# Seven products of combined halves in the output projection, with the combinations formed during the second half of the prompt, and a later place for DeltaNet's doubling

## The chip, the cores and the metric

The kernel runs on one core of one Trainium2 chip. TensorE (PE) multiplies and has its own weight loads (PEld); VectorE (DVE), ScalarE (ACT) and GpSimd (POOL) do the rest; transfers are issued from two queues, SyncE's (SP) and ACT's. The metric is the time of one execution in microseconds (us). Three runs of the kernel before took 2514.7, 2506.16 and 2504.16 us, median 2506.16; the profiled execution took 2504.23 us, with a span of 2502.5 us.

## What is computed

One decoder layer on a prompt of 1024 tokens (with 16 meta tokens in front) and on 64 sample tokens (8 sequences of 8), width 2048, in float32:

```python
h = _rmsnorm(x, norm_w)
proj = jnp.einsum('bld,de->ble', h, w_in)          # 2048 x 8984: all q, k, v, gates, z
# 16 heads of 128: 6 mLSTM (A), 6 gated DeltaNet (B), 4 HGRN2 (C); each a scan over chunks with a state
hcat = jnp.concatenate([ha, hb, hc], axis=2)
hcat = hcat * lax.rsqrt(jnp.mean(hcat * hcat, axis=-1, keepdims=True) + EPS)     # per head
y = hcat.reshape(bsz, L, MIX) * out_norm_w * jax.nn.silu(z)
out = jnp.einsum('ble,ed->bld', y, w_out)          # 2048 x 2048
return x + out, (states ...)                        # then a last _rmsnorm with final_norm_w
```

DeltaNet needs a triangular solve of 64x64 in each chunk: `lax.linalg.triangular_solve(M, rhs, left_side=True, lower=True)`.

## The kernel before

**Products in float32.** Every factor is split in two parts, hi (cast to fp32r) and lo (the rest), and a product is three matmuls: hi x hi, lo x hi, hi x lo. A weight is loaded in pieces of 128x512 (256 KB) on ACT's DMA queue into `wraw` (5 buffers); ACT casts `whi`, DVE subtracts `wlo`. `next_piece` hands out a piece, `feed_ahead` splits three pieces ahead and loads seven ahead. A piece serves 12 matmuls of 512 columns in the second half.

**Stages.** The prompt is done in two halves of 512 tokens. Half 0 holds also the 64 samples and the meta tokens. For each half the input projection runs through all heads in the order of `ORDER` (tiles `acc`, from `hA` or `hB`); as the tiles of a head are done, `done_tile` starts the head's scan. Scan matmuls go on PE between the projection's. At a head's end `finish` takes the head norm (`hr`, with a power on POOL), multiplies with `silu(z)` (`zs`), splits `y` into hi and lo and stores both in DRAM (`y_dram`). The output projection stands behind the second half's input projection: for half 0 four groups of 512 columns, 16 heads each, four token tiles and the samples; then half 1 the same. Its accumulators are `oacc`. `load_y` reads `y` back; the residual `x` is added from tiles `res`, squares are summed on ACT, POOL multiplies with `fnw` (the final norm's weights), and `final_norm` scales and stores the rows, among the following group's matmuls.

**What sets the order.** The order of the program is written by a planner of the kernel's own. A `Clock` holds an estimated time for each engine; `Weave` holds queues of generators, `scan`, `fin` (finishes), `post` and `bg`. Between two matmuls of a projection `pump` lets the heads of the queues go on whose due time has come by PE's clock T. `drain` moves T forward until some streams are done. `start_head` keeps at most two heads open: for the next it drains the oldest one's scan and all finishes in the queue. A scheduler then lays the instructions out engine by engine; each engine works in that order and waits for semaphores. All engine operations are recorded in one helper, L137, so they are told apart by tiles.

**DeltaNet.** `gdn_scan` builds `Ball` (decay times k k), writes its diagonal blocks to DRAM (`db`, eight transfers on SP, L1209) and reads them back spread over the partitions (`Bb`, three transfers, L1215). On DVE the substitution works on the 16x16 blocks: 15 pairs `Yt<-Yc,Bb` and `Yc<-Yc,Yt`, then `Y`, transposed to `X`. The doubling follows, from 16 to 32 to 64 and beyond: `pz<-X,Ball` on PE, an evacuation to `s`, `pyy<-Y,s` on PE, a subtraction, the next stage. The planner puts the substitution at `ready` = T + 7 us or later and the doubling 8 us behind the substitution's end.

## Time and profile before

| | |
|---|---|
| runs | 2514.7, 2506.16, 2504.16 us |
| profiled execution | 2504.23 us, span 2502.5 us |
| PE busy | 2439.2 us (97%) |
| DVE, ACT, POOL busy | 58%, 40%, 22% |
| moved | 350.81 MB, mean 140 GB/s |
| output projection | from about 2100 us to the end, 1664 matmuls |

The page names engines, tiles and, behind "<-", what ended an idle time. PE's share of 97% means that PE's order and its waits set the time; other engines count where PE waits for them.

### The profile page before, as it was taken

What the parts mean: (1) busy time and instruction counts of PE and PEld (TensorE: products, weight loads), DVE (VectorE), ACT (ScalarE), POOL (GpSimd) and SP (SyncE); (2) the same over time, 40 slices, a digit from 0 to 9 for tenths busy, and PEclk for the clock granted to TensorE, in tenths of its full rate; (3) what the DMA queues carried; (4) which work ended last, traced back from release to release, by engine and by line L of the source; (5) the groups of instructions that cost most, each with busy time, mean ns of one, the idle gap of its engine ahead of it and who ended that gap; (6) DMA issues with size and microseconds to landing.
All of it is one profiled execution on the core that took longest, in us unless ns stands there. A gap on an engine that the chain in (4) does not pass through costs nothing.

```text
span 2502.5 us, 43732 instructions
## 1 busy us (share of the span) xinstructions
PE 2439.2 (97%) x16032; PEld 2182.3 (87%) x16032; DVE 1439.8 (58%) x3080; ACT 992.7 (40%) x2428; POOL 553.6 (22%) x743
## 2 busy tenths in 40 slices
PE   6989999999999999999999999999999999999998
PEld 5988999999999999998787888888888888888886
DVE  7775665764647656555854556554654546333435
ACT  5733434443434334343642334333533334222324
POOL 5331212421204312123320114110320102111201
PEclk9999999999999999999999999999999999999999
DMA  6656666655545445448445455454544559536735
GB/s 149 159 128 154 159 151 150 161 121 124 129 104 140 99 124 138 105 111 227 121 122 119 117 124 131 120 133 101 142 119 112 132 124 308 135 82 203 248 101 181
DMA packets 681043, 350.81 MB, mean 140 GB/s; under 512 B 260004, under 2 KB 622076, under 8 KB 680828
## 3 DMA queue, kind: packets, MB, share of 16 engines
q10 hardware_dynamic: 318528, 185.64, 29.4%
q1 hardware_dynamic: 362300, 162.37, 25.1%
q8 instruction: 126, 2.06, 0.3%
q14 instruction: 89, 0.73, 0.1%
HBM read 285.71 MB, written 62.19 MB: 139 GB/s over the span
## 4 chain that ended last, share of the span: by engine, by line
PE 78%; DVE 7%; DMA 6%; issue 3%; ACT 2%; POOL 2%; SPq 2%; ACTq 0%; DVEq 0%; POOLq 0%
PE acc L137 54%; PE oacc L137 13%; DVE wlo L137 2%; PE pa L137 1%; SPq L1209 1%; DMA wraw<-in_w_in_dram 1%; DMA Bb<-db 1%; PE po L137 1%; PE pyy L137 1%; PE nd L137 1%; PE pu L137 1%; PE pz L137 1%; DVE Yt L137 1%; PE poh L137 1%; DVE Yc L137 1%
## 5 line engine op out<-in xcount | busy, mean ns | idle before, releaser
L137 DVE TENSOR_TENSOR wlo<-wraw,whi 128x512 fp32r<-128x512 f32 x720 | 536.8, 747 | 559.4 <-ACT whi L137 527.0
L137 PE MATMUL acc<-hA,whi 128*128 128x288 f32 (+1 forms) x4544 | 821.0, 303 | 5.3 <-DVE whi L137 5.1
L137 ACT CAST whi<-wraw 128x512 fp32r<-128x512 f32 x720 | 443.6, 618 | 945.4 <-PE acc L137 463.3
L137 PE MATMUL acc<-hB,whi 128*128 128x512 f32 x2272 | 724.8, 401 | 3.8 <-DMA hB<-hblo 3.3
L137 PEld LDWEIGHTS acc<-hA,whi 128*128 128x128 f32 x4544 | 676.1, 190 | 10.4 <-issue 6.9
L137 PEld LDWEIGHTS acc<-hB,whi 128*128 128x128 f32 x2272 | 414.9, 190 | 86.4 <-DMA hB<-hblo 4.0
L137 PE MATMUL acc<-hA,wlo 128*128 128x288 f32 x2240 | 487.9, 298 | 2.0 <-DVE wlo L137 1.8
L137 PE MATMUL acc<-hB,wlo 128*128 128x512 f32 x1120 | 441.0, 394 | 1.3 <-DVE wlo L137 1.3
L137 PEld LDWEIGHTS acc<-hA,wlo 128*128 128x128 f32 x2240 | 365.7, 189 | 3.3 <-DVE wlo L137 3.3
L137 PE MATMUL oacc<-whi,y 128*128 128x512 f32 x1088 | 343.0, 390 | 1.0 <-ACT whi L137 1.0
L137 PEld LDWEIGHTS acc<-hB,wlo 128*128 128x128 f32 x1120 | 211.5, 189 | 49.1 <-DVE wlo L137 3.6
L137 PEld LDWEIGHTS oacc<-whi,y 128*128 128x128 f32 x1088 | 204.3, 188 | 43.7 <-ACT whi L137 1.7
L137 PE MATMUL oacc<-wlo,y 128*128 128x512 f32 x576 | 224.7, 390 | 2.0 <-DVE wlo L137 2.0
L137 PEld LDWEIGHTS oacc<-wlo,y 128*128 128x128 f32 x576 | 108.2, 188 | 25.6 <-DVE wlo L137 3.6
L137 POOL TENSOR_TENSOR res<-res,fnw 128x512 f32<-128x512 f32 (+1 forms) x34 | 48.6, 1457 | 258.1 <-ACT oscr L137 258.1
L137 POOL TENSOR_TENSOR y<-y,zs 128x592 fp32r<-128x592 f32 (+1 forms) x32 | 45.9, 1435 | 155.5 <-ACT zs L137 152.6
L137 POOL TENSOR_TENSOR qd<-qT,emb 128x512 f32<-128x512 f32 x12 | 17.8, 1480 | 232.3 <-PE po L137 232.3
L137 DVE TENSOR_TENSOR Yt<-Yc,Bb 128x60 f32<-128x60 f32 (+8 forms) x180 | 36.9, 205 | 46.2 <-DMA Bb<-db 40.9
L137 POOL TENSOR_TENSOR hr<-hr,halfneg 128x4 f32<-128x4 f32 (+1 forms) x48 | 46.5, 969 | 67.4 <-DVE hr L137 66.1
L137 POOL TENSOR_TENSOR nrm<-nrm,halfneg 128x10 f32<-128x10 f32 x12 | 23.4, 1954 | 143.4 <-DVE nrm L137 126.8
L137 POOL TENSOR_TENSOR X<-Ex,hk 128x256 f32<-128x256 f32 (+1 forms) x40 | 41.4, 1035 | 56.6 <-PE pa L137 48.2
L137 DVE TENSOR_TENSOR Sx<-Sx,lf 128x256 f32<-128x256 f32 (+2 forms) x60 | 36.3, 609 | 23.1 <-ACT Ex L137 21.2
(416 smaller groups left out, 2755.5 us busy)
## 6 DMA issues: line engine op xcount, KB each, us to landing
wraw<-in_w_in_dram ACTq DMA_DIRECT2D x564, 256.0 KB
wraw<-in_w_out_dram ACTq DMA_DIRECT2D x144, 256.0 KB
y<-y SPq DMA_DIRECT2D x16, 576.0 KB
px<-in_x_prompt_dram SPq DMA_DIRECT2D x32, 256.0 KB
yd<-y SPq DMA_DIRECT2D x128, 64.0 KB
out_dram<-sst SPq DMA_DIRECT2D x16, 512.0 KB
s<-yd SPq DMA_DIRECT2D x32, 256.0 KB
y<-zs SPq DMA_DIRECT2D x32, 256.0 KB
```

The costliest lines, as they stand in the source:

```text
L137: return f(out, *a, **k)
L1209: DMA(db[j], Ball[SUB * j:SUB * (j + 1), 0:C, SUB * j:SUB * (j + 1)])
```

## The change

The output projection is done as one product of 2x2 blocks in the form of Strassen and Winograd. The rows' blocks are the two halves of the prompt, the columns' blocks column groups 0, 1 and 2, 3, and the inner blocks two sets of eight heads: K1, the first eight in the order of the input projection, and K2. There are seven products, numbered 1 to 7 here: A11·B11, A12·B21, S2·T2, S1·T1, S4·B22, S3·T3, A22·T4. Each has two column groups, eight pieces and four tiles; the samples, which are computed plainly, go along in the first three. Partial sums are held in tiles `t1` and `q`, copied and added by ACT, DVE and POOL, and the residuals are added on POOL in `x_added`.

The S are sums and differences of `y` of both halves. `finish` of half 0 also stores `y` whole; `finish` of half 1 loads this, forms the combinations on POOL, splits each on ACT and DVE, and stores them: three stores for a head of K1 (and one load), eight for a head of K2 (and three loads). The T are combinations of blocks of `w_out`. A background stream in half 1, `combine_weights`, forms them in 16 rounds: four loads of 256 KB on SP, which are kept behind all that precedes them in the source, four subtractions on POOL, four stores to DRAM on SP. `gdn_scan`'s two numbers rise from 7 to 10 and from 8 to 11.

Counted over the program, PE has 10809 rows (before 10951), POOL 795 (692), SP 850 (593), DVE 2728 (2643).

```diff
-OUT_UNITS = ([(cg, range(5)) for cg in range(4)], [(cg, range(4)) for cg in range(3)] + [(3, range(2)), (3, range(2, 4))])
+HEADS = [{"A": 0, "B": HA, "C": HA + HB}[name[0]] + int(name[1]) for name in ORDER[1:]]
+K1, K2 = HEADS[:NH // 2], HEADS[NH // 2:]
+LAST_UNITS = [(0, range(4)), (1, range(2)), (1, range(2, 4))]
...
+        if not half.first:
+            DMA(ya, y_whole[0][K1[kk]])
+            if not upper:
+                DMA(yb, y_whole[1][kk])
+                DMA(yc, y_whole[0][head])
...
+        if half.first:
+            S.copy(yhi[:, 0:W], y[:, 0:W])
+            ck.last += 1.0
+            yield
+            DMA(y_whole[0][head], y[:, 0:HALF])
+            ck.last = ck.t["T"] + 2.0
+            yield
+            G.tensor_tensor(ylo[:, 0:W], y[:, 0:W], yhi[:, 0:W], op=ALU.subtract)
...
+        def parts(src, hi, name):
+
+            S.copy(hi, src)
+            ck.sync()
+            V.tensor_tensor(src.bitcast(F32R), src, hi, op=ALU.subtract)
+            d = y_comb[name][kk].bitcast(F32)
+            ck.last = max(ck.last, ck.t["T"]) + 3.0
+            yield
+            DMA(d[:, 0:HALF], hi.bitcast(F32))
+            DMA(d[:, HALF:], src)
+
+        if upper:
+            G.tensor_tensor(ya, ya, y, op=ALU.subtract)
+            ck.last += 1.0
+            yield
+            DMA(y_whole[1][kk], y)
+            yield from parts(ya, yhi, "S3")
+            return
+        G.tensor_tensor(yb, yb, y, op=ALU.add)
+        yield
+        yield from parts(y, yhi, "A22")
+        G.tensor_tensor(ya, yb, ya, op=ALU.subtract)
+        yield
+        yield from parts(yb, spare, "S1")
...
-        ready = ck.t["T"] + 7.0
+        ready = ck.t["T"] + 10.0
...
-        ck.last += 8.0
+        ck.last += 11.0
...
+    def combine_weights():
+        for j in range(2):
+            for kk in range(NK // 2):
+                b11, b12, b21 = (sp.tile([P, 512], F32, tag="px", name="px", bufs=3) for _ in range(3))
+                b22 = sp.tile([P, 512], F32, tag="pxs", name="pxs", bufs=1)
+                for t, heads, cg in ((b11, K1, j), (b12, K1, j + 2), (b22, K2, j + 2), (b21, K2, j)):
+                    tc.keep_in_program_order(DMA(t, i["w_out"][0, P * heads[kk]:P * (heads[kk] + 1), 512 * cg:512 * (cg + 1)]))
+                for dst, a, b in ((b11, b12, b11), (b12, b22, b12), (b22, b22, b11), (b21, b21, b22)):
+                    ck.last = ck.t["T"] + 7.0
+                    yield
+                    G.tensor_tensor(dst, a, b, op=ALU.subtract)
+                ck.last = ck.t["T"] + 4.0
+                yield
+                for n, t in (("T1", b11), ("T3", b12), ("T2", b22), ("T4", b21)):
+                    DMA(w_comb[n][NK // 2 * j + kk], t)
+                ck.last = ck.t["T"] + 10.0
+                yield
...
+    each = every(0, "S4")
+    for j in range(2):
+        accs = banks()
+        phase(1, j, accs, halfn, each=each)
+        for n in halfn:
+            q[j, n] = free.pop(0)
+            ck.begin()
+            V.tensor_tensor(q[j, n], t1[j, n], accs[n], op=ALU.add)
+    weave.drain_queue("post")
+
+    each = every(1, "S3", [x_rows((4, 12), 1, 2), x_added(t1, 5, 0)])
+    for j in range(2):
+        accs = banks()
+        phase(0, j, accs, halfn, each=each)
+        for n in halfn:
+            t = res[n + 1, j + 2]
+            ck.begin()
+            V.tensor_tensor(t, t, accs[n], op=ALU.add)
+            G.tensor_tensor(t, t, q[j, n], op=ALU.add)
+            squared(n + 1, j + 2)
+    weave.add("post", final_norm(range(1, 5), range(4)))
...
```

The last two pieces are products 5 (S4) and 6 (S3).

How the instructions move shows at three places. The first is the doubling of DeltaNet's fifth head (B4) in half 1. On PE, before and then with the change (a name's number is its buffer; `acc` rows are the input projection of the heads behind):

```order
L137 MATMUL acc<-hB_14959,wlo 128x512
L137 MATMUL pz<-X_21883,Ball 32x32 x16
L137 MATMUL acc<-hB_14959,whi 128x512
L137 MATMUL acc<-hB_14960,whi 128x512
L137 MATMUL acc<-hB_14959,wlo 128x512
L137 MATMUL pyy<-Y_21882,s_22081 32x32 x16
L137 MATMUL acc<-hB_14743,whi 128x512
L137 MATMUL acc<-hB_14744,whi 128x512
L137 MATMUL acc<-hB_14743,wlo 128x512
L137 MATMUL acc<-hB_14743,whi 128x512
L137 MATMUL acc<-hB_14744,whi 128x512
L137 MATMUL acc<-hB_14743,wlo 128x512
```

```order
L137 MATMUL acc<-hB_14984,wlo 128x512
L137 MATMUL pz<-X_22222,Ball 32x32 x16
L137 MATMUL pyy<-Y_22221,s_22332 32x32 x16
L137 MATMUL pz<-X_22222,Ball 32x32 x8
L137 MATMUL pyy<-Y_22221,s_22378 32x32
L137 MATMUL pyy<-s_22378,Y_22221 32x32
...
L137 MATMUL pyy<-Y_22221,s_22378 32x32 x4
L137 MATMUL pz<-s_22358,Ball 64x64 x4
L137 MATMUL pyy<-s_22356,s_22427 64x64 x4
L137 MATMUL acc<-hB_14772,whi 128x512
L137 MATMUL acc<-hB_14773,whi 128x512
L137 MATMUL acc<-hB_14772,wlo 128x512
```

Before, three to eighteen `acc` matmuls stand between two stages; now the stages follow each other directly, up to the last `pyy`. On DVE at the same place, from the substitution's end, before and then with the change:

```order
L137 TENSOR_TENSOR Y_21882<-Yc,evenodd 128x128
L137 STREAM_TRANSPOSE X_21883<-Y_21882 128x128
L137 COPY Yc<-subid 128x64
L137 TENSOR_TENSOR wlo<-wraw,whi 128x512 x2
L137 TENSOR_TENSOR s_22081<-pz,lowleft 128x4x32
L137 STREAM_TRANSPOSE vT<-acc 128x512
L137 TENSOR_TENSOR Y_21882<-Y_21882,pyy 128x128
L137 TENSOR_TENSOR wlo<-wraw,whi 128x512
L137 STREAM_TRANSPOSE X_21883<-Y_21882 128x128
L137 TENSOR_TENSOR s_22105<-Y_21882,submask 128x512
L137 TENSOR_TENSOR wlo<-wraw,whi 128x512
L137 TENSOR_SCALAR s_22105<-pyy 32x4x32
```

```order
L137 TENSOR_TENSOR Y_22221<-Yc,evenodd 128x128
L137 STREAM_TRANSPOSE X_22222<-Y_22221 128x128
L137 COPY Yc<-subid 128x64
L137 TENSOR_TENSOR s_22332<-pz,lowleft 128x4x32
L137 TENSOR_TENSOR Y_22221<-Y_22221,pyy 128x128
L137 STREAM_TRANSPOSE X_22222<-Y_22221 128x128
L137 TENSOR_TENSOR s_22356<-Y_22221,submask 128x512
L137 TENSOR_SCALAR s_22356<-pyy 32x4x32
L137 TENSOR_SCALAR s_22358<-pyy 32x4x32
L137 TENSOR_SCALAR s_22356<-pyy 32x4x32
L137 TENSOR_SCALAR s_22356<-pyy 64x4x64
L137 SCALAR_TENSOR_TENSOR s_22240<-pr,cols,s_22240 128x128
```

The splits `wlo` of the projection's pieces, which stood between the stages, are ahead of them or behind them now. The second place is SP ahead of DeltaNet's first head (B0) in half 1, before and then with the change (`yd`, `y`, `yw`, `S` and `ya` belong to the finish of the head before, `T` are the stores of a round of combinations):

```order
L812 DMA yd_16185<-y 32x16x32 x4
L816 DMA s_16181<-yd_16185 128x4x128
L879 DMA y_767<-zs 128x512
L879 DMA y_767<-y 128x512
L1209 DMA db_16351<-Ball 64x1x16 x8
L785 DMA nm<-rows_765 128x512
L1215 DMA Bb<-db_16351 128x1x384 x2
L1215 DMA Bb<-db_16351 128x1x192
L785 DMA bb<-rows_765 128x512
```

```order
L844 DMA s_19076<-yd_19080 128x4x128
L1775 DMA T_82<-px 128x512
L1775 DMA T_84<-px 128x512
L1775 DMA T_83<-pxs 128x512
L1775 DMA T_85<-px 128x512
L948 DMA yw_92<-y 128x512
L941 DMA S_88<-zs 128x512
L942 DMA S_88<-ya 128x512
L899 DMA ya<-yw_91 128x512
L1289 DMA db_19301<-Ball 64x1x16 x8
L813 DMA nm<-rows_776 128x512
L1295 DMA Bb<-db_19301 128x1x384 x2
```

Four stores of combinations, which wait for POOL, and four transfers of the longer finish now stand ahead of `db`, where two stores stood. The third place is PE at an mLSTM head of half 0, before and then with the change:

```order
L137 MATMUL acc<-hA_88,wlo 128x288
L137 MATMUL acc<-hA_88,wlo 128x304
L137 MATMUL pot<-ident,tho 80x128
L137 MATMUL pum<-meta_731,kwall 128x137
L137 MATMUL pum<-s_5268,kwall 128x129 x4
L137 MATMUL acc<-hA_88,whi 128x288
L137 MATMUL acc<-hA_88,whi 128x304
L137 MATMUL acc<-hA_89,whi 128x288
L137 MATMUL acc<-hA_89,whi 128x304
L137 MATMUL acc<-hA_88,wlo 128x288
L137 MATMUL acc<-hA_88,wlo 128x304
```

```order
L137 MATMUL acc<-hA_99,wlo 128x304
L137 MATMUL pot<-ident,tho 80x128
L137 MATMUL pum<-meta_742,kwall 128x137
L137 MATMUL pum<-s_5305,kwall 128x129 x4
L137 MATMUL py<-ident,t_5210 128x80
L137 MATMUL nd<-sst,spread_740 32x129 x8
L137 MATMUL nd<-t_5294,t_5252 32x129 x2
L137 MATMUL nd<-t_5294,t_5252 16x129
L137 MATMUL nd<-state_A_758,qd 128x129
L137 MATMUL nd<-s_5305,s_5260 128x129
```

Where `pum` and `nd` had `acc` matmuls between them, they now follow each other; six heads of half 0 have this with the change, two had before.

338 lines of the change are left out of this document (243 added, 95 removed).

## The prediction

> **What bounds the kernel now.** I read the page first: the busy shares, the slices, and the shares of the chain of waits.
>
> ```profile
> PE 2439.2 (97%) x16032; PEld 2182.3 (87%) x16032; DVE 1439.8 (58%) x3080; ACT 992.7 (40%) x2428; POOL 553.6 (22%) x743
> ...
> PE   6989999999999999999999999999999999999998
> ...
> DMA  6656666655545445448445455454544559536735
> GB/s 149 159 128 154 159 151 150 161 121 124 129 104 140 99 124 138 105 111 227 121 122 119 117 124 131 120 133 101 142 119 112 132 124 308 135 82 203 248 101 181
> ...
> PE 78%; DVE 7%; DMA 6%; issue 3%; ACT 2%; POOL 2%; SPq 2%; ACTq 0%; DVEq 0%; POOLq 0%
> PE acc L137 54%; PE oacc L137 13%; DVE wlo L137 2%; PE pa L137 1%; SPq L1209 1%; DMA wraw<-in_w_in_dram 1%; DMA Bb<-db 1%; PE po L137 1%; PE pyy L137 1%; PE nd L137 1%; PE pu L137 1%; PE pz L137 1%; DVE Yt L137 1%; PE poh L137 1%; DVE Yc L137 1%
> ```
>
> TensorE (PE) is busy for 2439.2 of 2502.5 us, no slice after the second falls below 9 tenths, and the chain runs through PE for 78%. So a matmul taken away is worth its time, and anything new costs only if PE waits for it. In the output projection the groups of instructions and the windows say what one matmul is worth:
>
> ```profile
> L137 PE MATMUL oacc<-whi,y 128*128 128x512 f32 x1088 | 343.0, 390 | 1.0 <-ACT whi L137 1.0
> ...
> L137 PE MATMUL oacc<-wlo,y 128*128 128x512 f32 x576 | 224.7, 390 | 2.0 <-DVE wlo L137 2.0
> ```
>
> ```profile
> core 0: us, PE busy (x) PEld busy (x) DVE busy (x) ACT busy (x) POOL busy (x), PEclk, DMA share, GB/s
> 2000.00:2100.00 100.00, 100.00 (x583) 82.59 (x582) 48.16 (x113) 35.28 (x76) 9.16 (x13) 1.00 0.67 190
> 2100.00:2200.00 100.00, 100.00 (x503) 83.80 (x502) 45.55 (x70) 34.08 (x72) 25.02 (x23) 1.00 0.61 176
> 2200.00:2300.00 100.00, 100.00 (x443) 82.84 (x442) 32.79 (x44) 26.68 (x53) 14.54 (x10) 1.00 0.44 134
> 2300.00:2400.00 100.00, 98.73 (x435) 81.08 (x434) 40.39 (x70) 31.33 (x60) 16.92 (x14) 1.00 0.67 214
> ```
>
> The columns are the stretch, its length, busy time (and instructions) of PE, weight load, DVE, ACT and POOL, then the clock, the DMA share and GB/s. Between 2200 and 2300 us there is nothing but the output projection: 443 matmuls in 100 us, 0.2257 us each (the 390 ns of the groups overlap). It waits for almost nothing (1.0 and 2.0 us in the two groups). The waits of PE that the change touches:
>
> ```profile
> PE pz L137 <- DVE Yc L137: 4.0, 1, 4.0
> ...
> PE pz L137 <- DVE X L137: 2.7, 1, 2.7
> ...
> PE oacc L137 <- DVE wlo L137: 2.0, 3, 1.5
> ...
> PE nd L137 <- DVE nsT L137: 0.5, 1, 0.5
> ```
>
> **Part 1: fewer matmuls.** Before, the projection has 1088 + 576 = 1664. The seven products have 7 x 2 x 8 pieces x 4 tiles x 3 = 1344, the samples 128: 1472. 192 x 0.2257 = **-43.3 us**. All else on PE keeps its count.
>
> **Part 2: the doubling is placed later.** The two waits of `pz` (3.98 and 2.70 us, the first DeltaNet head of each half) are longer than they look, for the clock falls behind them:
>
> ```profile
> 225.00:230.00 5.00, 3.25 (x40) 3.05 (x40) 4.78 (x16) 1.14 (x2) 0.00 (x0) 0.64 0.44 108
> 230.00:235.00 5.00, 4.87 (x47) 4.53 (x46) 3.20 (x10) 2.01 (x7) 1.71 (x3) 0.50 0.80 136
> 235.00:240.00 5.00, 5.00 (x65) 4.51 (x64) 2.68 (x7) 1.78 (x7) 1.09 (x4) 0.83 0.22 56
> ...
> 1330.00:1335.00 5.00, 5.00 (x42) 4.01 (x41) 1.86 (x4) 0.28 (x1) 0.87 (x2) 0.50 0.38 96
> 1335.00:1340.00 5.00, 5.00 (x58) 3.44 (x57) 2.07 (x5) 1.14 (x3) 0.00 (x0) 0.92 0.19 22
> ```
>
> At clocks 0.50 and 0.83 the windows from 230 to 240 us lose 5 x 0.50 + 5 x 0.17 = 3.35 us; those from 1330 to 1340 lose 2.9. The planner now places the doubling 3 us later (+8 to +11). For head B0 of half 0 that takes 3.0 of 3.98 us and, with a wait near 1 us left, the clock's loss: 3.0 + 3.4 = **-6.4 us** (bounds 0 and -7.4). For head B0 of half 1 it would take 2.7 + 2.9 = 5.6 us, but the order shows a round of the weights' combinations ahead of its `db` rows on SP. Before, POOL and SP stood there so:
>
> ```profile
> 1298.35 1.96 POOL L137 TENSOR_TENSOR nrm<-nrm,halfneg 128x10 f32<-128x10 f32 x1 [11.00 <-DVE nrm L137]
> ```
>
> ```profile
> 1306.74 5.07 SPq L1209 DMA_DIRECT2D db<-Ball  x8
> ...
> 1314.07 1.90 SPq L1215 DMA_DIRECT2D Bb<-db  x3
> ```
>
> The four subtractions stand behind that `nrm` operation, which ends at 1300.3. Each costs what the nearest POOL row of 128x512 costs (the first row here):
>
> ```profile
> L137 POOL TENSOR_TENSOR res<-res,fnw 128x512 f32<-128x512 f32 (+1 forms) x34 | 48.6, 1457 | 258.1 <-ACT oscr L137 258.1
> ...
> L137 DVE TENSOR_TENSOR Yt<-Yc,Bb 128x60 f32<-128x60 f32 (+8 forms) x180 | 36.9, 205 | 46.2 <-DMA Bb<-db 40.9
> ```
>
> 1300.3 + 4 x 1.46 = 1306.1 us, when T4's store is released. Behind it on SP stand three stores of the head before and one load; the stores wait for one more POOL subtraction (1.5), a cast and a DVE subtraction (some 1.4). So `db` starts near 1310.5 instead of 1306.74, and `Bb` 3.8 us later. That eats the 3.4 us that `pz` moved back: **0** (bounds -5.6, if SP gets through, and +4, if a load lands late).
>
> **Part 3: head B4 of half 1.** The finishes of half 1 have become longer, and the planner's clock, which is made to wait for the oldest head, jumps just when this head's substitution runs. The order shows the result: `pz` and `pyy` stand in one block with no `acc` matmul between them, and the two rows of `wlo` that stood between the substitution's end and `s<-pz` before are gone, as are all up to the end of the doubling. Counted in the program from the first `Yt`, 56 matmuls (12.7 us) stood ahead of `pz` before and 11 (2.5 us) do now. Before, the trace has there:
>
> ```profile
> 2010.40 0.22 DVE L137 TENSOR_TENSOR Yt<-Yc,Bb 128x60 f32<-128x60 f32 x1 [4.20 <-DMA Bb<-db]
> ...
> 2018.99 0.31 DVE L137 STREAM_TRANSPOSE X<-Y 128x128 f32<-128x128 f32 x1
> ...
> 2021.64 0.28 DVE L137 TENSOR_TENSOR s<-pz,lowleft 128x128 f32<-128x128 f32 x1
> ```
>
> ```profile
> 2020.61 0.90 PE L137 MATMUL pz<-X,Ball 32*32 32x32 f32 x32
> ...
> 2022.32 0.89 PE L137 MATMUL pyy<-Y,s 32*32 32x32 f32 x32
> ...
> 2025.42 0.59 PE L137 MATMUL pz<-X,Ball 32*32 32x32 f32 x16
> ...
> 2031.83 0.68 PE L137 MATMUL pyy<-s,s 64*64 64x64 f32 x8
> ```
>
> X was ready at 2018.99 + 0.31 = 2019.30 and `pz` began at 2020.61, 1.3 us of slack. With 10.2 us less ahead of it PE waits 10.2 - 1.3 = 8.9 us. Then come five hand-offs without cover. From `pz` at 2020.61 the evacuation began 1.03 us later, took 0.28, and `pyy` followed 0.4 us behind it: some 1.7 us for a pair in which PE works 0.9. With ACT's and POOL's copies in the later ones I take 0.9 us of idle PE each, 4.7 in all. An idle of 9 us also costs clock: by the two instances above, 3.4 us. Sum **+17.0 us**. Bounds: 8 (Bb there at once, no loss of clock) and 25 (1.5 us a hand-off, DVE's splits between, 5 us of clock).
>
> The Trainium skill (TensorE: Matmul & The Clock Gate, Why this matters for your kernels) says to keep gaps of PE under about 3 us, or the clock drops to half. The trace agrees and is harsher: the 2.70 us wait already brought 0.50. By the rule only B4's first wait costs clock, which is what I took; without the rule the sum would be 3.4 us lower.
>
> **Part 4: half 0.** Finishes yield twice more and write `y_whole`. On PE six of the mLSTM heads now have `pot`, `pum`, `nd`, `pu` with no `acc` between, two before. The rows of such a wait are 0.5 us (`nd <- nsT`): 4 to 5 more of them, **+2.5 us** (0 to 5). The 16 more stores lie on SP, and nothing waits for them before half 1.
>
> **Part 5: weights' combinations.** 64 loads, 64 stores and 64 subtractions in half 1: 33.5 MB in some 1000 us, 34 GB/s beside the 101 to 142 of those slices: hidden. 64 x 1.46 = 93 us on POOL, busy 22%. What costs is order: each round holds POOL for the loads plus 5.8 us, and SP until then. Of the other `db` rows none has a round within 8 us ahead. DVE waits for POOL's powers in `finish`, but these are off PE's path until the planner drains. **+2 us** (0 to 10).
>
> POOL's work also slows DVE's split:
>
> ```profile
> 2084.96 0.69 DVE L137 TENSOR_TENSOR wlo<-wraw,whi 128x512 fp32r<-128x512 f32 x1 [2.03 <-ACT whi L137]
> ...
> 2089.34 1.37 DVE L137 TENSOR_TENSOR wlo<-wraw,whi 128x512 fp32r<-128x512 f32 x1 [1.21 <-DMA wraw<-in_w_out_dram]
> ```
>
> ```profile
> 2088.87 1.30 POOL L137 TENSOR_TENSOR y<-y,zs 128x512 fp32r<-128x512 f32 x1 [16.62 <-ACT zs L137]
> ```
>
> The split takes 0.69 us alone and 1.37 under a POOL operation. With 103 more POOL rows that is at most 70 us of DVE, busy 58%, and splits are made three pieces (8.1 us) ahead: nothing on the path. The Trainium skill (GPSIMD Engine Reference, 8. Key points) names the cause, SBUF interfaces shared with VectorE. Taken as a price on the path, 64 x 0.68 = 44 us, it would eat the whole saving; I don't, because `oacc` waited 2.0 us for `wlo` in all while POOL was busy 25 us in 100.
>
> **Part 6: the output stage's epilogue.** Behind products 5 and 6 POOL has 12 operations for a column pair, 17.5 us against 192 / 2 x 0.2257 = 21.7 us. DVE's scaling of the rows of tiles 1 to 4 waits for POOL's power, and the split of a later piece stands behind it; the cover is 8.1 us. I take **+4 us** (0 to 12) for this, the six banks of a column pair of product 2, and the end.
>
> **Part 7: transfers.** Products 1 to 3 (704 matmuls, 158.9 us) read 80 pieces (21.0 MB), S2 and S1 (8.4), x (2.1), and the last heads' finishes move some 8.6: 40.1 MB, 252 GB/s. The windows show 214 GB/s at a share of 0.67 and 176 at 0.61, so 290 to 320 at 1.0, and one slice had 308 while PE didn't wait. It fits, with little room: **+2 us** (0 to 20).
>
> Sum: -43.3 - 6.4 + 0 + 17.0 + 2.5 + 2 + 4 + 2 = -22.2. The profiled execution took 2504.2 us, 1.9 below the median: 2482.0 there, **2484 us** as a median.
>
> **Rivals.** *No jam at B4*: the runtime order absorbs it (Bb earlier, DVE free of splits). For: DVE has no splits to do there. Against: PE's order is fixed. Without the 17.0: 2467 us. *The output stage runs at the speed of DMA*: at 240 GB/s the 40.1 MB take 167 us, at 220 182: 8 to 23 us, less the 2 counted: about 2498. For: before, this stage never had more than 214 over 100 us. Against: the 308 slice. *The epilogue binds*: POOL's column pairs leave 4 us; if splits wait at each of three, 12 us instead of 4: 2492. *The combinations hold SP and POOL ahead of DeltaNet*: one mechanism at each `Bb` of half 1. If loads land 8 us late, the store rows hold SP as at B0, and all six heads stall 3 us more and lose 3 us of clock: 2484 + 38 = 2522. It decides from the point where a round ends later than its `db`'s place; the rows give the other five 8 us or more. *The change doesn't do what it says*: the order has the 192 matmuls less, so this has no weight.
>
> **How the numbers follow.** Forecast 0.45, no jam 0.20, DMA 0.13, epilogue 0.12, SP and POOL 0.10. About 0.5% (12.5 us) is what a measurement here can tell from no change, so faster means below 2493.6. The forecast's own range is 2472 to 2496; nearly all of it, the no-jam case and half of the epilogue's are faster: 0.70. DMA, the rest of the epilogue's and of the forecast's are within: 0.21. Slower: 0.09. The range for 8 in 10 reaches from the no-jam case (2467, with epilogue and transfers free 2461) into the DMA case's upper end: 2461 to 2507.
>
> **What would show it.** Right: 0.226 us per matmul in the products; a wait of `pz` for DVE of 7 to 11 us in half 1's fifth DeltaNet head, with the clock at 0.5 behind it; no such wait in the first head of half 0; one of 2 to 4 us still in the first head of half 1; `Bb` issued some 4 us later there. Wrong: `oacc` waiting for DMA or `wlo` by more than 10 us in products 1 to 3; POOL's subtractions ahead of a DeltaNet wait elsewhere; `pz` at B4 without a wait.

## The result: slower by 2.4%

The changed kernel takes 2566.48 us (median of 2563.59, 2563.84, 2569.11 and 2571.99), the kernel before, beside it, 2509.39 us: a ratio of 1.0239 (95% interval 1.0220 to 1.0258), 57 us slower. The forecast was 2484, its range 2461 to 2507. Both miss, and on the other side.

The profiled execution of the changed kernel took 2571.99 us, the longest of the four. Its page, in the parts that answer those shown of before:

```profile
PE 2435.8 (95%) x15840; PEld 2164.0 (84%) x15840; DVE 1525.0 (59%) x3160; ACT 1022.8 (40%) x2476; POOL 711.6 (28%) x855
...
PE   6989999999999999998999999999987999899988
...
PE 22%; DMA 5%; DVE 3%; issue 3%; POOL 3%; ACT 1%; SPq 1%; ACTq 0%; POOLq 0%; DVEq 0%
```

PE has fewer instructions (15840 for 16032) but is busy as long as before (2435.8 and 2439.2 us): what is left runs at a lower clock. There are slices of 8 tenths in the second half. The chain of waits can't be compared: followed back from the end it breaks off at 1558 us, so its shares add up to 38% of the span, and PE's 22% is not to be held against the 78% of before. PE's four largest groups of waits (behind each the total, the count and the longest; before, `oacc` waited 2.0 us for `wlo`):

```profile
PE acc L137 <- DVE wlo L137: 16.3, 15, 2.4
PE pz L137 <- DVE X L137: 14.7, 3, 11.9
PE pyy L137 <- DVE s L137: 11.5, 8, 2.6
PE oacc L137 <- DVE wlo L137: 11.2, 6, 5.6
```

Two kinds stand out: DVE's splits `wlo`, in the input projection and in the output projection (27.5 us), and DeltaNet's `pz` and `pyy` (26.2 us), with the longest single wait. To see where the time went I cut the span at the first `acc` matmul of half 1 behind half 0's last scan matmuls (80 of half 1's 3392 have run by then), at the last `acc`, and at the last `oacc`. "Waits" is PE's idle time in the stage.

| us | half 0 | half 1 | output stage | waits in each |
|---|---|---|---|---|
| before | 1202.0 | 898.4 | 391.2 | 44.8, 5.0, 3.0 |
| after | 1208.1 | 970.0 | 380.9 | 53.4, 46.5, 23.6 |

Half 1 lost 71.6 us. The output stage won 10.3 where 43.3 were due. A stage of a single execution is good to some 6 us: the changed kernel and ten of the kernels below have the same order on PE up to half 1's first `acc` matmul, and their half 0 took from 1203.2 to 1215.2 us. The windows that hold half 1 and most of the output stage, and two short ones that are used further down, of after and then of before (columns as in the prediction):

```profile
1208.10:2178.10 970.00, 923.54 (x4986) 749.85 (x4985) 549.04 (x1091) 364.43 (x840) 262.69 (x253) 0.96 0.62 170
2178.10:2490.00 311.90, 290.48 (x1291) 237.00 (x1290) 161.89 (x237) 112.76 (x219) 100.17 (x80) 0.97 0.77 249
2140.00:2200.00 60.00, 60.00 (x284) 50.44 (x283) 34.97 (x60) 26.56 (x52) 18.32 (x18) 1.00 0.91 309
2380.00:2440.00 60.00, 60.00 (x267) 49.67 (x266) 25.02 (x35) 14.32 (x24) 14.96 (x11) 1.00 0.72 232
```

```profile
1202.00:2100.40 898.40, 893.35 (x4985) 738.44 (x4984) 505.52 (x1064) 351.96 (x818) 161.07 (x183) 0.99 0.52 131
2100.40:2490.00 389.60, 386.59 (x1760) 319.50 (x1759) 164.61 (x248) 127.23 (x251) 72.21 (x59) 1.00 0.55 168
```

Half 1 has 46.5 - 5.0 = 41.5 us more of waits, and the same matmuls kept PE busy for 923.54 us instead of 893.35, 30.2 longer: that is the whole loss. The longer busy time goes with the clock, whose mean fell from 0.99 to 0.96: 0.04 x 970.0 - 0.01 x 898.4 = 30 us (good to some 5 us, since the clock is printed to two digits and some of the low clock falls into the waits themselves). The output stage likewise: 391.2 - 43.3 = 347.9, plus 20.6 of waits, plus some 11 of clock (0.97 for 1.00), makes 380; 380.9 were measured. So there is one question: what are the waits? In half 1 each costs about 1.7 times its length.

### The profile page after: what moved, and what is told of

It reads as the page before. It is cut to its first block, busy times and chain, and to the rows that moved or that the text cites. A ratio compares the mean times of both kernels' runs of the same rounds, so it can differ in the third digit from the quotient of the medians.

```text
span 2570.1 us, 44178 instructions
## 1 busy us (share of the span) xinstructions
PE 2435.8 (95%) x15840; PEld 2164.0 (84%) x15840; DVE 1525.0 (59%) x3160; ACT 1022.8 (40%) x2476; POOL 711.6 (28%) x855
## 5 line engine op out<-in xcount | busy, mean ns | idle before, releaser
L137 DVE TENSOR_TENSOR wlo<-wraw,whi 128x512 fp32r<-128x512 f32 x728 | 557.9, 770 | 544.7 <-ACT whi L137 486.0
L137 PE MATMUL acc<-hB,whi 128*128 128x512 f32 x2272 | 739.1, 405 | 7.1 <-DMA hB<-hblo 3.6
L137 PEld LDWEIGHTS acc<-hB,whi 128*128 128x128 f32 x2272 | 423.2, 192 | 93.9 <-ACT whi L137 6.2
L137 PE MATMUL oacc<-whi,y 128*128 128x512 f32 x928 | 300.5, 398 | 2.7 <-ACT whi L137 2.7
L137 PEld LDWEIGHTS oacc<-whi,y 128*128 128x128 f32 x928 | 178.1, 192 | 42.2 <-ACT whi L137 4.5
L137 PE MATMUL oacc<-wlo,y 128*128 128x512 f32 x480 | 191.4, 399 | 11.4 <-DVE wlo L137 11.2
L137 PEld LDWEIGHTS oacc<-wlo,y 128*128 128x128 f32 x480 | 92.3, 192 | 33.4 <-DVE wlo L137 14.1
L137 ACT ACTIVATE Wt<-pw,nrm 128x128 f32<-128x128 f32 (+1 forms) x54 | 19.8, 367 | 86.5 <-PE pw L137 76.2
L137 PE MATMUL pa<-X 128*128 128x128 f32 (+2 forms) x400 | 42.2, 254 | 12.0 <-ACT U L137 8.1
L137 PEld LDWEIGHTS pa<-X 128*128 128x128 f32 (+2 forms) x400 | 40.6, 166 | 15.2 <-ACT U L137 8.3
```

The source lines that it names most:

```text
L137: return f(out, *a, **k)
```

## The experiments

17 kernels were run, each beside runs of the kernel before on the same chip; the ratio is to these. Unless said otherwise a kernel does all the work.

| kernel | us | ratio to before | half 0, half 1, output stage | waits in half 1, output stage |
|---|---|---|---|---|
| after | 2566.48 | 1.0239 [1.0220, 1.0258] | 1208.1, 970.0, 380.9 | 46.5, 23.6 |
| comb_only | 2541.24 | 1.0137 [1.0120, 1.0155] | 1202.8, 936.5, 389.8 | 29.1, 1.9 |
| no_comb | 2524.35 | 1.0073 [1.0052, 1.0093] | 1208.9, 922.7, 378.8 | 23.1, 24.9 |
| no_sub | 2544.84 | 1.0146 [1.0121, 1.0171] | 1210.1, 941.6, 380.7 | 34.9, 24.0 |
| short_finish | 2561.04 | 1.0214 [1.0187, 1.0241] | 1212.3, 953.6, 380.0 | 35.3, 26.3 |
| pin_subs | 2578.31 | 1.0274 [1.0249, 1.0299] | 1212.8, 974.5, 378.9 | 53.7, 21.3 |
| out_later | 2565.09 | 1.0228 [1.0203, 1.0252] | 1211.8, 962.9, 376.5 | 47.3, 22.0 |
| all_three | 2555.46 | 1.0191 [1.0165, 1.0218] | 1210.1, 949.1, 381.4 | 35.9, 24.2 |
| dve_sub | 2549.83 | 1.0168 [1.0144, 1.0192] | 1215.0, 942.4, 380.1 | 31.6, 25.4 |
| out_dve | 2545.50 | 1.0161 [1.0125, 1.0197] | 1215.2, 972.3, 359.3 | 52.2, 9.8 |
| no_comb_short | 2514.52 | 1.0028 [1.0010, 1.0047] | 1203.2, 916.2, 383.4 | 13.4, 26.9 |
| v2 | 2510.70 | 1.0024 [1.0013, 1.0034] | 1208.6, 929.3, 359.0 | 22.0, 9.8 |
| lag_only | 2506.16 | 0.9997 [0.9982, 1.0011] | 1203.7, 898.9, 390.8 | 3.1, 2.4 |
| old_lag | 2591.87 | 1.0343 [1.0305, 1.0380] | 1219.7, 975.4, 376.9 | 58.5, 23.1 |
| v2_lag | 2523.31 | 1.0068 [1.0045, 1.0091] | 1220.4, 933.7, 357.3 | 25.7, 8.5 |
| v2_early | 2541.20 | 1.0135 [1.0103, 1.0166] | 1261.2, 905.5, 361.3 | 8.4, 11.0 |
| v3_pool | 2534.80 | 1.0105 [1.0087, 1.0122] | 1235.8, 926.7, 361.8 | 22.0, 10.6 |
| v3 | 2502.62 | 0.9986 [0.9975, 0.9998] | 1220.9, 910.0, 358.3 | 10.9, 9.3 |

### The weights' combinations: left out, without their subtractions, and alone

```diff
 no_comb:  the stream is left out
-            weave.add("bg", combine_weights())
 no_sub:  the subtractions alone are left out
-                    G.tensor_tensor(dst, a, b, op=ALU.subtract)
 comb_only:  the kernel before, with the stream added
+            weave.add("bg", combine_weights())
```

> The changed kernel without combine_weights: the 64 loads, 64 subtractions and 64 stores of half 1 are left out, and the pieces of T1 to T4 are read from one place of w_out, same size and count, so y is not the layer's output. PE's order is the changed kernel's, the jam at B4 included. Theory A (the rounds of combinations hold POOL and SP, ACT waits for POOL and the casts behind it come late): half 1 loses its 60 to 70 us; time 2490 to 2510. Theory B (the longer finishes and the transfers of the output stage do it): the combinations are worth under 20 us; 2545 to 2565.

> The changed kernel with all loads and stores of combine_weights, but without its 64 POOL subtractions: T1 to T4 hold plain blocks of w_out, so y is not the layer's output. Theory A with POOL as the culprit (its queue waits for the loads, and HGRN's and finish's work stands behind): nearly all of the gain of leaving the rounds out, 2495 to 2515. Theory A with SP's queue or the transfers as the culprit: little of it, 2540 to 2565.

> The kernel before with combine_weights added in half 1 and its results unused; the output projection, the finishes and the two numbers of gdn_scan are those of before. Theory A: slower than before by 40 us or more, 2545 to 2575, by waits of PE for wlo in half 1. Theory B: within 15 us of before.

Without the stream the change takes 2524.35 us, 42 less, between the ranges of the two theories. On the kernel before, alone, the stream costs 33 us, nearly all in half 1 (+38.1). About half of the 42 goes with the 64 subtractions, 2566.48 - 2544.84 = 21.6; the other half, 20.5, stays with the loads and stores, so that no_sub lies in the range of its second theory. PE's waits in half 1 divide in the same way. For the splits (`wlo`, `whi`) PE waits 16.1 us in the change, 6.1 in no_sub and 5.4 in no_comb; for DeltaNet's `pz` and `pyy` 24.3, 23.2 and 17.0; for HGRN's `pcn` and `puh` 4.7, 4.9 and 0. So the subtractions show at the splits, the loads and stores at DeltaNet and HGRN. The part that I called hidden is most of the loss. But the change without it is still 0.7% slower than before: the output stage's missing saving is not touched by it (378.8 us).

### Three theories on the planner and the order: all small or wrong

My theories were that the finishes' longer waiting times let the planner jam B4, that POOL sits waiting for loads just issued, and that the output stage's sums come too early in the order.

```diff
 short_finish:  shorter waiting times in finish, half 1
-        ck.last = ck.t["T"] + 5.0
+        ck.last = ck.t["T"] + (5.0 if half.first else 4.0)
-            ck.last = max(ck.last, ck.t["T"]) + 3.0
+            ck.last = max(ck.last, ck.t["T"])
 pin_subs:  the subtractions keep the source's place, not the loads
-                    tc.keep_in_program_order(DMA(t, i["w_out"][...]))
+                    DMA(t, i["w_out"][...])
-                    G.tensor_tensor(dst, a, b, op=ALU.subtract)
+                    tc.keep_in_program_order(G.tensor_tensor(dst, a, b, op=ALU.subtract))
 out_later:  the samples' sums and final_norm some pieces later
-    sample_add(0, held, False)
-    sample_add(1, sacc, False)
+    each = every(0, "S2", [x_rows((5, 10), 1, 0), samples_later], (6, 9, 12))
-    weave.add("post", final_norm(range(1, 5), range(4)))
+    each = every(0, "A22", [x_added(q, 5, 2), norm_later])
 all_three:  the three together
```

> The changed kernel with the planner's 3 us behind each hi/lo split of a finish in half 1 taken away, and one wait of 5 us made 4: the same work, but the planner's clock doesn't jump at head B4, and 48 acc matmuls stand again between its first Yt and pz, and some between its stages. If the jam at B4 costs what the trace of the change shows there (11.9 + 0.7 + 0.8 us of waits and a low clock behind them), the time falls by 14 to 20 us, to 2546 to 2553. If SP and POOL are late there anyway, or the jam only moves, by less than 7.

> The changed kernel with the subtractions of combine_weights held in the source's place on POOL, and the loads free to move instead: the loads of a round now stand 20 us or more ahead of its subtractions. All work is kept. If what hurts is that POOL stands still for loads that were just issued, with HGRN's exponents on ACT and the casts behind them, half of the 42 us that the rounds cost comes back: 2535 to 2550. If it is the transfers or the 93 us of POOL's work itself, under 10 us: 2556 to 2570. Slower if the loads are now ahead of DeltaNet's transfers.

> The changed kernel with two things of the output stage put later: the additions of the first two column groups' samples, from ahead of product 2 to behind its fourth piece, and the final norm of tiles 1 to 4, from behind product 6 to five pieces later. If the waits there are what the trace shows (ACT held by DVE, DVE by the load of x for the samples: 5.6 us and 3.9 us with a low clock behind; DVE by POOL's power: 5.6 and 1.4 us), the output stage falls from 381 to some 360 us, the time to 2545 to 2552. If the stage is bound by the transfers, it stays within 6 us.

> The three together. If the causes are separate, the gains add up: 2566 less 17, 20 and 18, about 2510, the same as before. If one of them only moves into another, 2525 or more.

short_finish undoes the jam: the waits of `pz` for DVE fall from 14.7 to 2.1 us. Half 1 of its profile is 16.4 us shorter, but its median is only 5.4 us lower and the two intervals overlap: somewhere between 5 and 16. pin_subs is not faster than the change (1.0274 against 1.0239), so POOL's waiting for loads just issued is not what the subtractions cost. out_later changes nothing; the scheduler puts the sums back. Together they give 11 us of 57.

The traces of these kernels show what the waits are. In all_three, DVE and then POOL (start, duration, engine, operation):

```profile
1823.15 1.79 DVE L137 TENSOR_TENSOR y<-y,zs 128x512 fp32r<-128x512 f32 x1
1824.86 1.77 DVE L137 SCALAR_TENSOR_TENSOR lf<-cf,Lr 128x512 f32<-128x512 f32 x1
...
1828.27 0.68 DVE L137 TENSOR_TENSOR lf<-lf,ur 128x512 f32<-128x512 f32 x1
```

```profile
1824.35 1.74 POOL L137 TENSOR_TENSOR pxs<-pxs,px 128x512 f32<-128x512 f32 x1
1826.05 1.75 POOL L137 TENSOR_TENSOR yc<-yc,ya 128x512 f32<-128x512 f32 x1
```

```profile
1832.87 0.50 PE L137 MATMUL acc<-hB,wlo 128*128 128x512 f32 x1 [3.43 <-DVE wlo L137]
```

While POOL works on two inputs, DVE's operations on 128x512 take 1.77 to 1.79 us; `lf<-lf,ur`, behind POOL's last, takes 0.68. The next split stands behind them and behind an operation that waits 1.05 us for POOL's `hr`, and PE idles 3.43 us. Only one of POOL's four operations in a row there belongs to the weights, the others are the finish's combinations; no_comb, without the weights', still has a wait of 2.54 us for a split, beside a finish's combinations (at 1827.92). This is the Trainium skill's rule (GPSIMD Engine Reference, 8. Key points: GpSimd and VectorE share SBUF interfaces) that the prediction named and set aside; the trace agrees, and adds the size. A second path, in the changed kernel, goes through ACT:

```profile
1883.11 1.28 POOL L137 TENSOR_TENSOR px<-px 128x512 f32<-128x512 f32 x1 [4.79 <-DMA px<-in_w_out_dram]
...
1887.21 1.28 POOL L137 TENSOR_TENSOR px<-px,pxs 128x512 f32<-128x512 f32 x1
1888.45 0.72 POOL L137 TENSOR_TENSOR X<-Ex,hk 128x256 f32<-128x256 f32 x1
1889.13 0.72 POOL L137 TENSOR_TENSOR X<-Ex,hq 128x256 f32<-128x256 f32 x1
```

```profile
1889.88 0.63 ACT L137 ACTIVATE eP<-lf 128x512 f32<-128x512 f32 x1 [9.88 <-POOL X L137]
1890.41 0.60 ACT L137 CAST whi<-wraw 128x512 fp32r<-128x512 f32 x1
```

```profile
1891.05 1.28 DVE L137 TENSOR_TENSOR wlo<-wraw,whi 128x512 fp32r<-128x512 f32 x1 [9.68 <-ACT whi L137]
```

```profile
1891.55 0.38 PE L137 MATMUL pcn<-ident,U 128*3 128x128 f32 x1 [3.48 <-ACT U L137]
```

POOL had been idle 4.79 us for the loads; its four subtractions then hold it from 1883.11 to 1888.5 us. Behind them stand the two products `X` of an HGRN head, and ACT waits 9.88 us in all until these are done. Behind that stand ACT's cast `whi`, with DVE's split behind the cast, and ACT's copy `U`, for which PE idles 3.48 us. This wait doesn't need the subtractions. At the same place of no_sub, POOL and then ACT:

```profile
1858.70 0.64 POOL L137 TENSOR_SCALAR_AFFINE_SELECT bb<-bb 128x512 f32<-128x512 f32 x1 [6.71 <-DMA px<-in_w_out_dram]
```

```profile
1862.14 0.63 ACT L137 ACTIVATE eP<-lf 128x512 f32<-128x512 f32 x1 [8.50 <-POOL X L137]
```

POOL idles 6.71 us, by the profile for a load of the round, `X` stands behind that, and ACT waits 8.50 us for it. In the output stage of the changed kernel the same chain starts from POOL's adds:

```profile
2461.08 4.44 POOL L137 TENSOR_TENSOR res<-res 128x512 f32<-128x512 f32 x3 [8.06 <-DMA wraw<-T]
```

```profile
2465.55 0.63 ACT L137 ACTIVATE oscr<-res 128x512 f32<-128x512 f32 x1 [1.90 <-POOL res L137]
...
2469.92 0.60 ACT L137 CAST whi<-wraw 128x512 fp32r<-128x512 f32 x1
```

```profile
2472.26 1.32 DVE L137 TENSOR_SCALAR res<-res,fr 128x512 f32<-128x512 f32 x3 [3.11 <-POOL fr L137]
...
2474.97 1.68 DVE L137 TENSOR_TENSOR wlo<-wraw,whi 128x512 fp32r<-128x512 f32 x1
```

```profile
2476.70 0.79 PE L137 MATMUL oacc<-wlo,y 128*128 128x512 f32 x1 [5.62 <-DVE wlo L137]
```

ACT squares each row as POOL's add delivers it, its cast for the next piece stands behind these, at 2469.92, and DVE's split behind the scaling of rows that waited 3.11 us for POOL's power: PE idles 5.62 us. The first such place of the stage has another cause, a load:

```profile
2233.93 0.68 DVE L137 TENSOR_TENSOR res<-res,oacc 64x512 f32<-64x512 f32 x1 [7.70 <-DMA res<-in_x_sample_dram]
```

```profile
2236.40 2.08 PE L137 MATMUL puh<-s,s 128*128 128x128 f32 x8 [5.62 <-ACT s L137]
```

DVE's sum for the samples waits 7.70 us for the samples' `x`, with everything of DVE behind it, and PE idles 5.62 us. POOL's work stands in three of the four paths, a late load in two of them.

### Taking the work from POOL

```diff
 dve_sub:  the weights' subtractions on DVE, their loads not held
-                    tc.keep_in_program_order(DMA(t, i["w_out"][...]))
+                    DMA(t, i["w_out"][...])
-                    G.tensor_tensor(dst, a, b, op=ALU.subtract)
+                    tc.keep_in_program_order(V.tensor_tensor(dst, a, b, op=ALU.subtract))
 out_dve:  the output stage's sums on DVE; the samples' x is added later, in product 3
-            G.tensor_tensor(t, t, t1[j, n], op=ALU.add)
+            V.tensor_tensor(t, t, t1[j, n], op=ALU.add)
-            G.tensor_tensor(t, t, q[j, n], op=ALU.add)
+            V.tensor_tensor(t, t, q[j, n], op=ALU.add)
-        res[0, cg] = x_load(0, cg)
+        res[0, cg] = free.pop(0)
 no_comb_short:  no_comb with short_finish
 v2:  short_finish, dve_sub and out_dve, and the finishes' combinations on DVE
-        G.tensor_tensor(yb, yb, y, op=ALU.add)
+        V.tensor_tensor(yb, yb, y, op=ALU.add)
...
```

> The changed kernel with the 64 subtractions of the weights' combinations on DVE, held in the source's place, their loads free to move ahead. Theory A (POOL is what hurts: its time, and DVE's slower work beside it): as without the subtractions, 2540 to 2552. Theory B (SP's queue and the transfers of the rounds hurt, whoever subtracts): 2555 to 2575. If DVE now waits for the loads, slower still.

> The changed kernel; in the output stage the additions of t1 and q to the rows move from POOL to DVE, and the samples' residual is added in product 3 instead of waited for ahead of product 2. Theory A (ACT's squares wait for POOL's additions one by one, with the casts behind them; DVE waits for the samples' x with the splits behind it): the 5.6 and 5.6 us waits and the low clock behind them go, the stage falls from 381 to 360 to 368 us, the time by 12 to 20 us, to 2546 to 2555. Theory B (the transfers bind the stage, with 230 to 310 GB/s): the waits move to the pieces' loads and the stage stays within 5 us of 381.

> The changed kernel without combine_weights (T1 to T4's pieces are read from one place of w_out, so y is not the layer's output) and with the short finishes that undo the jam at B4. What is left against the kernel before is the longer finishes of half 1, the output stage and half 0. If the rounds and the jam are the two causes in half 1, half 1 takes 900 to 912 us (898 before) and the time is 2503 to 2514; if the finishes cost more by themselves, 2515 to 2525.

> The changed kernel with all of this: short finishes, the rounds' subtractions and the finishes' combinations on DVE, the output stage of out_dve. If POOL is the common cause, the gains add up to 45 us or more and the time is 2505 to 2525, that is near the kernel before; if SP's queue is, 2535 to 2555.

dve_sub against pin_subs is the cleanest pair: the same loads, the subtractions held in place in both, only the engine differs. It is 2578.31 against 2549.83, and by the ratios 1.0274 against 1.0168: about 27 us for 64 operations (17 against the change itself, 2566.48). On DVE they cost hardly more than left out (half 1 942.4 us, in no_sub 941.6; medians 2549.83 and 2544.84). out_dve brings the output stage from 380.9 to 359.3, 32 of the 43.3 us due. Its median is 21 us lower, with half 1 as it was. It makes two changes, POOL's sums and the samples' `x`, which were not run apart; the wait of 5.62 us that each had is gone. no_comb_short lies between its two theories (half 1 916.2 us), with ten runs from 2503.64 to 2525.04: beside the rounds and the jam, the longer finishes of half 1 cost something by themselves, 17.8 us in this execution. v2 does all the work and takes 2510.70, 0.24% slower than before where the change is 2.39%: of the 57 us some 53 are gone.

### The later doubling

```diff
 lag_only:  the kernel before, with the change's two numbers
+        ready = ck.t["T"] + 10.0
+        ck.last += 11.0
 old_lag, v2_lag:  the changed kernel and v2, with the old two numbers
+        ready = ck.t["T"] + 7.0
+        ck.last += 8.0
```

> The kernel before with the change's two numbers for DeltaNet's doubling alone (7 to 10 and 8 to 11); all work is kept. My Part 2 says that without the combinations' rows this takes the waits of pz in the first DeltaNet head of each half (3.98 and 2.70 us) down to near 1 us and 0, with the clock lost behind them: 6.4 + 5.6 = 12 us less, about 2496. A rival: a wait moves to the next hand-off of the doubling (pyy, as the profile of the changed kernel hints with 2.6 us there), and the time stays within 3 us of the kernel before. A second rival: the longer doubling makes the planner hold the next head back, some 5 to 10 us more.

> The changed kernel with DeltaNet's two numbers as they were (7 and 8); all work is kept. If the later place is worth what I predicted, this is 6 us slower than the change, 2573. If it is worth nothing, 2566 within 4. If the later place adds to the jam in the second half, where the finishes are longer, this is faster, 2550 to 2560.

> The kernel v2 (all work kept; combinations of weights and of y on VectorE, the output stage's sums on VectorE, short hi/lo finishes) with DeltaNet's two numbers as they were (7 and 8). v2 took 2510.7. If the later place of the doubling is what is left of the loss in the second half (929 us against 898), 2495; if it is worth 6 us, 2517; if nothing, 2511 within 4.

On the kernel before the later doubling is worth nothing: 2506.16 for 2507.04. `pz` of the first head in half 0 no longer waits, but the next step does, `pyy`, with the clock behind it as before. In the first head of half 1 the wait of 2.70 us is gone and 0.89 stand at `pyy`, but half 1 is no shorter (898.9 us for 898.4). PE's wait in half 0 of lag_only, and the window behind it:

```profile
234.18 1.35 PE L137 MATMUL pyy<-Y,s 32*32 32x32 f32 x32 [2.47 <-DVE s L137]
```

```profile
235.00:240.00 5.00, 5.00 (x46) 4.59 (x43) 3.73 (x9) 2.58 (x8) 1.94 (x3) 0.50 0.86 160
```

In the change, however, it is worth 25 us (2591.87 without it), and in v2 13. Most of what the profiled executions show of this lies in half 0: 11.6 us in old_lag and 11.8 in v2_lag, for 5.4 and 4.4 in half 1. There `pz` waits for the substitution in three heads of old_lag, 7.33, 3.38 and 4.46 us, where the change has 0.85 at `pz` and 2.62 at `pyy`. PE's waits of this kind in old_lag:

```profile
PE pz L137 <- DVE Yc L137: 15.7, 4, 7.3
```

Why the change needs the later place in half 0, where the kernel before does without, no run isolates. In half 1 the longest wait is at B4. DVE, SP and PE of old_lag:

```profile
1947.65 1.12 DVE L137 SCALAR_TENSOR_TENSOR Ball<-pkk,nrm,Ball 128x128 f32<-128x128 f32 x4
...
1958.65 0.22 DVE L137 TENSOR_TENSOR Yt<-Yc,Bb 128x60 f32<-128x60 f32 x1 [8.69 <-DMA Bb<-db]
```

```profile
1948.80 5.07 SPq L1289 DMA_DIRECT2D db<-Ball  x8
```

```profile
1966.14 1.35 PE L137 MATMUL pz<-X,Ball 32*32 32x32 f32 x32 [22.42 <-DVE X L137]
```

Eleven transfers of finishes stand ahead of `db` on SP, but it doesn't wait for them: it starts 0.03 us behind the end of `Ball`. In the changed kernel the same eleven stand there, and `db` starts 0.02 us behind `Ball`, at 1943.56. What differs is PE's order. In the changed kernel 48 `acc` matmuls (10.9 us) stand between `pvb`, the product ahead of the doubling, and `pz`, in old_lag none, and PE waits 22.42 us for 11.85. lag_only came out as its first rival said; no case that I had foreseen for old_lag and v2_lag had their size.

### Place or engine

v2_early puts v2's rounds of weights' combinations in half 0, ahead of the preparation of half 1's input (`prep_B`); v3 puts them right behind it. v3_pool is v3 with the combinations of weights and of `y` on POOL and the loads held, as in the change.

```diff
 v2_early
-            weave.add("bg", combine_weights())
+            if half.first and n == 3:
+                weave.add("bg", combine_weights())
 v3, v3_pool
-            weave.add("bg", combine_weights())
-                weave.add("bg", prep_B())
+                prep = weave.add("bg", prep_B())
+                weave.add("bg", combine_weights())
-                    weave.drain_queue("bg")
+                    weave.drain(prep)
```

> The kernel v2 with the 16 rounds of the weights' combinations in the first half of the prompt in place of the second; all work is kept. My theory now is that what is left of v2's loss are late transfers and VectorE's queue in the second half, where the rounds meet the longer finishes (waits 2.1, 3.4, 1.9, 4.9 and 5.8 us there). Then the second half falls from 929 to about 912 us, as in the kernel without combinations, the first half rises by 0 to 8, and the time is 2495 to 2504. The rival: the rounds cost the first half what they cost the second, since the cost is VectorE's and SP's time itself, and the time stays at 2511 to 2520.

> The kernel v2 with the rounds of the weights' combinations directly behind prep_B, the preparation of the second half's input, whose last transfers stood at 514 us in the kernel before, so that they run from about 515 to 1190 us; all work is kept. In v2_early the rounds stood ahead of prep_B, which held the second half's input back (waits of 15.0 and 8.2 us for hB), and the second half fell to 905.5 us. My theory (the rounds cost where they meet the longer finishes and the DeltaNet heads of the second half): first half 1209 to 1218, second half 905 to 912, output stage 359 to 362, 2485 to 2500, 0.3 to 0.9% under the kernel before. The rival (the rounds cost the first half what they cost the second): first half near 1230, and 2505 to 2515.

> The kernel v3 with the combinations of the weights and of y on POOL, as in the change, and their loads held in the source's place; all work is kept. If the engine is what costs (POOL slows VectorE's two-input operations and ACT waits for POOL in HGRN), it is 20 to 30 us slower than v3, the first half above all. If the place is what costs (rounds beside the longer finishes), it is within 6 us of v3.

v2_early misses by a mistake of mine: the background queue works one stream after the other, so the input of half 1 came too late, and PE waited for it:

```profile
1201.15 1.19 PE L137 MATMUL acc<-hB,whi 128*128 128x512 f32 x2 [15.03 <-DMA hB<-hbhi]
```

Its half 1, without the rounds, takes 905.5 us. v3, without that mistake, takes 2502.62 us, 0.14% under the kernel before (interval 0.02 to 0.25%): the only kernel here that beats it, and by less than one would call a gain. v3_pool takes 2534.80. So at one and the same place POOL costs 32 us more (in the profiles 15 in half 0, 17 in half 1, 3 in the output stage). The loads' place differs as well, but pin_subs let them go without a gain. PE's waits for the split in the input projection, both halves, v3_pool and then v3:

```profile
PE acc L137 <- DVE wlo L137: 15.1, 11, 3.8
```

```profile
PE acc L137 <- DVE wlo L137: 6.3, 7, 2.1
```

The place matters less: v2 to v3 is 8 us, since half 1 fell by 19.3 and half 0 rose by 12.3; v3 lies between the ranges of its two theories. How much of the 32 us is DVE's slowing, and how much engines waiting in line behind POOL, no run tells apart: both end when POOL is relieved.

## Why the prediction was wrong

By stages the profiled execution is 90 us above the sum's 2482.0: half 1 by 53, the output stage by 27, half 0 by 10.

**Part 1 (fewer matmuls): right.** From 2380 to 2440 us PE is busy 60.00 us for 267 matmuls, 0.2247 us each; 0.2257 was the price. The -43.3 us were there, and were spent again.

**Part 2 (the later doubling): wrong.** "3.0 of 3.98 us and the clock's loss" for the first head of half 0 is a subtraction from one wait; the wait went to the next hand-off (0.85 us left at `pz`, 2.62 at `pyy`), and lag_only measures 0 where I had 12 without the rounds. The move itself was mis-sized, 3 us in one sentence and 3.4 in another: in half 1 102 to 105 `acc` matmuls stand between `pvb` and `pz` in lag_only, 75 to 78 before, which is 6 us. For the first head of half 1 the 2 to 4 us foreseen are 2.1, but by luck: SP doesn't hold `db` back. In all six heads of half 1 `db` starts 0.03 to 0.06 us behind the end of `Ball`, before and after. What is late is `Ball`, on DVE (in v2 and v3, where it comes earlier, `db` of the first head does start 2.5 and 2.3 us behind it). DVE at the first head, before and then with the change, and POOL with the change:

```profile
1300.34 0.16 DVE L137 TENSOR_TENSOR nrm<-nrm 128x5 f32<-128x5 f32 x1 [2.07 <-POOL nrm L137]
...
1305.59 1.12 DVE L137 SCALAR_TENSOR_TENSOR Ball<-pkk,nrm,Ball 128x128 f32<-128x128 f32 x4
```

```profile
1314.41 1.24 DVE L137 TENSOR_TENSOR nrm<-nrm 128x5 f32<-128x5 f32 x1 [2.07 <-POOL nrm L137]
...
1317.47 1.76 DVE L137 SCALAR_TENSOR_TENSOR y<-s,onw,zs 128x512 f32<-128x512 f32 x1
...
1323.97 1.12 DVE L137 SCALAR_TENSOR_TENSOR Ball<-pkk,nrm,Ball 128x128 f32<-128x128 f32 x4
```

```profile
1317.08 1.61 POOL L137 TENSOR_TENSOR pxs<-pxs,px 128x512 f32<-128x512 f32 x1
```

From `nrm` to the end of `Ball` DVE took 6.4 us, now 10.7. Four of its operations, `nrm`, two splits and `y`, run beside the four subtractions and take 1.0 to 1.1 us longer each. That the step is worth 25 us inside the change I did not see at all.

**Part 3 (the jam at B4): right in mechanism and size, in the trace.** DVE and PE in the changed kernel, and the windows:

```profile
1955.90 0.22 DVE L137 TENSOR_TENSOR Yt<-Yc,Bb 128x60 f32<-128x60 f32 x1 [5.67 <-DMA Bb<-db]
```

```profile
1964.66 1.35 PE L137 MATMUL pz<-X,Ball 32*32 32x32 f32 x32 [11.85 <-DVE X L137]
```

```profile
1960.00:1965.00 5.00, 0.34 (x8) 0.34 (x10) 4.06 (x21) 0.00 (x0) 0.30 (x1) 0.50 0.22 52
1965.00:1970.00 5.00, 3.55 (x91) 3.15 (x91) 1.46 (x4) 0.51 (x2) 0.87 (x2) 0.50 0.00 0
1970.00:1975.00 5.00, 3.71 (x39) 3.14 (x35) 1.27 (x4) 0.37 (x1) 0.00 (x0) 0.50 0.02 5
1975.00:1980.00 5.00, 5.00 (x18) 4.15 (x17) 0.35 (x1) 0.72 (x2) 0.00 (x0) 0.59 0.00 0
```

11.85 us of first wait (forecast 8.9) come from a late `Bb` too: DVE had been idle 5.67 us for it. The wait is the finishes' own: no_comb, without the rounds, has 11.67 us there. Behind the wait PE runs at 0.50 for over 10 us; at half clock the busy 3.55, 3.71 and 5.00 us lose 1.8 + 1.9 + 2.1 (at 0.59) = 5.7 us, and 2.7 are idle: 20 us against 17.0 (where five hand-offs of 0.9 stand as 4.7 instead of 4.5). Undone, it gave 5 to 16.

**Part 4 (half 0): too small.** Half 0 was to be 3.9 us shorter with Part 2 and is 6.1 us longer, 8 in the median of the eleven executions that have its order on PE. lag_only's is 1.7 longer; what makes up the rest no run isolates.

**Part 5 (the combinations, "hidden", +2 us): the step that failed.** Alone they cost 33 us, in the change 42. I reasoned from averages: POOL busy 22%, DVE 58%, splits three pieces ahead, `oacc` waiting 2.0 us for `wlo` with POOL busy 25%. But the waits come from moments. About half of the 42 goes with the subtractions: where four POOL operations in a row meet a DVE with several operations of 128x512 in a row, each of these takes 1.76 to 1.79 us instead of some 0.7, and the cover of 8.1 us is gone; PE then waits for the splits. The other half goes with the loads and stores, and shows as waits at DeltaNet and HGRN; one way is the load that POOL idles for ahead of HGRN's `X`, the rest no run isolates. I had looked for POOL's queue only at `db`, not at HGRN's `X` with ACT's cast behind. The sentence with 44 us, which I gave and rejected, was for the subtractions alone, which cost 17 to 27 us by no_sub, dve_sub and pin_subs; that it lies near the 42 of the whole stream is luck. And no part priced the longer finishes of half 1 beside the jam (17.8 us in no_comb_short).

**Part 6 (the epilogue, +4 us): failed, by the same cause.** The stage gave back 33 us. I compared sums, 17.5 us of POOL under 21.7 us of matmuls, where ACT's casts stood in line behind each POOL result. out_dve removes 21.6 of it, with the samples' `x`, at which I had not looked at all.

**Part 7 (transfers): right.** From 2140 to 2200 us 309 GB/s were moved with PE busy 60.00 us. But one wait is a transfer's, the 5.62 us behind the late `x` of the samples; I had priced the amount and not the time that a single load takes in the queue.

**The rivals.** DMA as the bound (0.13) falls with that window. The epilogue (0.12) was the right place, at a third of its price. The rival that came nearest, combinations holding SP and POOL (0.10, 2522), had the right sign. But SP holds no `db` of half 1, and I gave it DeltaNet's heads alone, which have 24.3 of the 46.5 us that PE waits in half 1, more than half of them the jam. PE waits 70 us in half 1 and the output stage; splits, DeltaNet, HGRN and the output stage's sums make up most of it, and the clock behind them adds some two thirds again. I gave "slower" 0.09 because each of these terms, taken by itself, had cover.
